# A macaron encoder layer on one core: another order of seven products, six plain tiles, an embedding norm elsewhere, other first loads

## The chip, the core and the metric

The kernel runs on one core of a Trainium2 chip. The metric is the time of one execution on the device in microseconds (us). The engines are named TensorE (PE in the profile, its weight loads PEld), VectorE (DVE), ScalarE (ACT), GpSimd (POOL) and SyncE (SP, which only issues DMAs here).

## What is computed

One layer of a bidirectional encoder for 512 positions of width 1024, all in fp32:

```python
h = h + 0.5 * swiglu(rms_norm(h, g_ffn1), w_ffn1_gate, w_ffn1_up, w_ffn1_down)   # width 2816
u = rms_norm(h, g_mix) @ w_in
h = h + concat([o_mla(u), o_diff(u)]) @ w_out
h = h + 0.5 * swiglu(rms_norm(h, g_ffn2), w_ffn2_gate, w_ffn2_up, w_ffn2_down)
gate = sigmoid(rms_norm(h, g_ple_in) @ w_ple_gate + b_ple_gate)
h = h + gate * rms_norm(p @ w_ple_proj, g_ple_out)
```

swiglu is (silu(u @ w_gate) * (u @ w_up)) @ w_down. The change touches the two feed-forward blocks, the product p @ w_ple_proj (the embedding product), its norm, and the start.

## The kernel before

**Precision.** Each fp32 operand is split into a high part (a cast to fp32r on ScalarE) and a low part (a subtraction on VectorE); `split`, lines 91 to 93. One product is three matmuls: high by high, high by low, low by high (`mm3`, lines 250 to 253). Everything is held transposed: features on the partitions, the 512 positions along the columns, so h is 8 tiles of 128x512.

**Weights.** All weights lie in one stream, read in order. `load_chunk` (line 106) loads a block of 128x1024 (512 KB) on SP's queue and splits it; there are 3 raw buffers and 5 of split blocks. `load_unit` (line 118) makes seven weight forms out of two such blocks, with two DMAs that add into SBUF (issued by GpSimd, lines 127 and 128) and two sums on GpSimd (lines 131 and 132): xa holds the blocks A11 and A12, xb S1 and A22, xc S3, xs S2 and S4. `nxt` (line 138) keeps about three blocks, or one unit, loaded ahead.

**Feed-forward block** (`ffn`, line 397). The 22 tiles of 128 inner columns come in three groups, `FGROUPS` (line 23): first tile, tiles, plain tiles. A plain tile is 24 matmuls of 512 columns for the gate and 24 for the up product (`proj`). The other tiles come in pairs: a pair is two runs of `seven` (line 359), one for the gate and one for the up product (here called the gate run and the up run). A run takes 7 products instead of 8, each of 4 x 3 matmuls of 256 columns (12). After the tiles of a group come 8 down products (`ps_d`), which are added to h.

A run of `seven` has three accumulators in PSUM, r1, r2 and r3, one bank each. A bank is read between the products that accumulate into it, and the next product into it waits for that reading. The order is

```python
mul(r1, A11, F_.B11, True, True)     # then ScalarE copies r1 to q1 lo (line 378)
mul(r3, S1, F_.N1, True, True)       # then VectorE adds r3 (line 381)
mul(r2, S2, F_.T2, True, True)       # then VectorE: q1 hi = q1 lo - r2 (line 384)
mul(r1, A12, F_.B21, False, True)
mul(r2, S3, F_.N3, False, True)      # then line 388 reads r2
mul(r3, S4, F_.B22, False, True)     # then line 391 reads r3
mul(r2, A22, F_.N4, False, True)     # then line 394 reads r2
```

The seven forms of the second operand (B11, N1, T2, B21, N3, B22, N4; class `Forms`, line 306) are built once for each block out of h, its gain and the row scale. The building is a generator of 18 steps, 9 for each half of the rows, started in the second plain tile; 6 steps are taken after each plain tile (line 453). The row scale comes from the sum of squares of h (`Norm`, line 234, summed in `square_sum`, lines 195 to 201), a reduction by matmuls (`col_rsqrt`, line 208), a power on GpSimd (line 183) and a broadcast by matmuls (`row_bcast`, line 226).

**Start.** SP's queue loads p (2 tiles), the first block of embedding weights, 4 tiles of x, the second block, 4 tiles of x, and tables. The 8 embedding products are evacuated in turn by VectorE and ScalarE into `pe` (4 pages of two tiles) and stored in DRAM. `pe_norm` (line 293) squares them on ScalarE and sums on GpSimd; it is the `side` generator of the first block, one step after each plain tile. The sum of the first norm is on VectorE (line 267). Table products for the rotary part (lines 542 to 548) are 24 small multiplications on GpSimd.

**What sets the order.** TensorE's instructions run in the order in which the code gives them. Those of the other engines are put in order by a scheduler from the code's order and their readiness; `tc.high_priority(offset=n)` moves some n places ahead. Each engine then works strictly in its order.

## Time and profile before

| | |
|---|---|
| median of 3 runs | 1090.54 us (1088.35 to 1092.55) |
| the profiled execution | 1091.32 us, its span 1089.5 us |
| TensorE busy | 1025.6 us, 94% of the span |
| VectorE, ScalarE, GpSimd busy | 69%, 47%, 29% |
| DMA | 131.25 MB, mean 120 GB/s |

The profile follows one execution. "Busy" is the time in which an engine ran an instruction; matmuls overlap, so the distance between the starts of two of them tells their pace. A timeline row gives the start, the duration, engine, line and operands, and in brackets the idle time before it with what ended it. The granted clock is the share of TensorE's full clock in a stretch; it has two levels, 1.2 and 2.4 GHz.

### The profile page before, as it was taken

To read this page: it belongs to the slowest core of one execution; us is meant where nothing else is said; L and a number is where in the kernel's file an instruction comes from. 1 tells how busy PE (TensorE), PEld (TensorE's weight loads), DVE (VectorE), ACT (ScalarE), POOL (GpSimd) and SP (SyncE) were. 2 spreads that over 40 slices of the span, in tenths; PEclk is the share of its full clock that TensorE was granted. 3 is DMA by queue.
4 is the path that set the end of the run, shared out by engine and by line. 5 is a ranking of instruction groups with operands and counts; after the bars stand their busy time and mean duration, and the time that the engine had idled before them with its cause. 6 is when DMAs were issued, how large, how long until landed. Compare 5 with 4: busy or idle time off the path is not lost.

```text
span 1089.5 us, 15824 instructions
## 1 busy us (share of the span) xinstructions
PE 1025.6 (94%) x6056; PEld 898.4 (82%) x6056; DVE 750.3 (69%) x1216; ACT 509.2 (47%) x811; POOL 317.3 (29%) x304
## 2 busy tenths in 40 slices
PE   7788999999999999998889999969999999999998
PEld 5677989998898989886458888869889998999886
DVE  7488735886368656888878865887537874487673
ACT  8444423544144444657787744443325442344441
POOL 2743113340134030004454314332023511241330
PEclk9897999999999999999899999979999999999999
DMA  8524643766355443221200023335636655364441
GB/s 313 172 68 107 173 124 106 173 151 194 97 132 139 146 165 104 86 98 58 78 20 1 21 66 100 91 101 132 178 79 163 165 163 139 106 162 115 136 149 49
DMA packets 47580, 131.25 MB, mean 120 GB/s; under 512 B 5520, under 2 KB 6160, under 8 KB 47504
## 3 DMA queue, kind: packets, MB, share of 16 engines
q1 hardware_dynamic: 34560, 105.04, 29.6%
q0 software_dynamic: 11648, 23.07, 11.9%
q10 hardware_dynamic: 1296, 2.13, 0.5%
q8 instruction: 47, 0.77, 0.3%
q14 instruction: 29, 0.24, 0.1%
HBM read 123.93 MB, written 6.29 MB: 120 GB/s over the span
## 4 chain that ended last, share of the span: by engine, by line
PE 73%; DVE 13%; issue 5%; ACT 4%; DMA 3%; POOL 2%; SPq 0%; ACTq 0%; POOLq 0%; DVEq 0%
PE r L251 9%; PE r L252 8%; PE r L253 8%; PE ps_d L252 7%; PE ps_d L251 7%; PE ps_d L253 7%; PE ps_in L251 2%; PE ps_in L253 2%; PE ps_in L252 2%; DMA rc<-in_wst_dram 2%; DVE y L328 1%; DVE xb L93 1%; PE ps_pg L251 1%; PE ps_pg L253 1%; PE ps_wo L251 1%
## 5 line engine op out<-in xcount | busy, mean ns | idle before, releaser
L92 ACT CAST hl<-raw 128x1024 fp32r<-128x1024 f32 (+4 forms) x100 | 98.9, 992 | 167.0 <-issue 72.9
L93 DVE TENSOR_TENSOR hl<-raw,hl 128x1024 fp32r<-128x1024 f32 (+4 forms) x100 | 116.3, 1166 | 45.4 <-ACT hl L92 45.0
L252 PE MATMUL ps_d<-ht,hl 128*128 128x512 f32 x352 | 137.2, 390 | 0.0
L251 PE MATMUL ps_d<-ht,hl 128*128 128x512 f32 x352 | 137.0, 389 | 0.0
L253 PE MATMUL ps_d<-ht,hl 128*128 128x512 f32 x352 | 136.9, 389 | 0.0
L128 POOL DMA_DIRECT2D rc<-in_wst_dram x36 | 31.2, 867 | 205.9 <-DMA rc<-in_wst_dram 132.7
L251 PE MATMUL r<-fm,xb 128*128 128x256 f32 x288 | 84.8, 295 | 5.9 <-ACT fm L92 5.9
L252 PE MATMUL r<-fm,xb 128*128 128x256 f32 x288 | 82.8, 288 | 5.6 <-DVE fm L93 5.6
L252 PE MATMUL r<-fm,xa 128*128 128x256 f32 x288 | 82.3, 286 | 3.8 <-DVE fm L93 3.8
L251 PE MATMUL r<-fm,xa 128*128 128x256 f32 x288 | 82.2, 285 | 2.6 <-ACT fm L92 2.6
L251 PE MATMUL r<-fm,xs 128*128 128x256 f32 x288 | 82.9, 288 | 0.0
L252 PE MATMUL r<-fm,xs 128*128 128x256 f32 x288 | 82.8, 288 | 0.0
L253 PE MATMUL r<-fm,xs 128*128 128x256 f32 x288 | 82.7, 287 | 0.0
L253 PE MATMUL r<-fm,xb 128*128 128x256 f32 x288 | 82.5, 287 | 0.0
L253 PE MATMUL r<-fm,xa 128*128 128x256 f32 x288 | 82.1, 285 | 0.0
L92 ACT CAST xa<-ra 128x1024 fp32r<-128x1024 f32 x36 | 37.8, 1051 | 89.9 <-PE r L253 36.1
L252 PEld LDWEIGHTS ps_d<-ht,hl 128*128 128x128 f32 x352 | 66.1, 188 | 14.1 <-DVE ht L93 0.6
L253 PEld LDWEIGHTS ps_d<-ht,hl 128*128 128x128 f32 x352 | 66.1, 188 | 13.7
L251 PEld LDWEIGHTS ps_d<-ht,hl 128*128 128x128 f32 x352 | 66.1, 188 | 13.5
L127 POOL DMA_DIRECT2D rb<-in_wst_dram x36 | 31.5, 874 | 148.7 <-DVE h L465 51.4
L92 ACT CAST xs<-ra 128x1024 fp32r<-128x1024 f32 x36 | 37.7, 1048 | 78.3 <-PE r L253 54.3
L201 POOL TENSOR_TENSOR acc<-acc,sq 128x512 f32<-128x512 f32 x21 | 34.3, 1634 | 112.8 <-ACT sq L200 112.8
(324 smaller groups left out, 2998.7 us busy)
## 6 DMA issues: line engine op xcount, KB each, us to landing
raw<-in_wst_dram SPq DMA_DIRECT2D x77, 512.0 KB, 3.5
rb<-in_wst_dram SPq DMA_DIRECT2D x36, 512.0 KB, 3.6
ra<-in_wst_dram SPq DMA_DIRECT2D x36, 512.0 KB, 3.6
rc<-in_wst_dram SPq DMA_DIRECT2D x36, 256.0 KB, 4.4
rb<-in_wst_dram POOLq DMA_DIRECT2D x36, 256.0 KB, 4.0
rc<-in_wst_dram POOLq DMA_DIRECT2D x36, 256.0 KB, 4.6
raw<-in_wst_dram SPq DMA_DIRECT2D x16, 384.0 KB, 3.1
h<-in_xT_dram SPq DMA_DIRECT2D x8, 256.0 KB, 6.7
```

What stands on the lines that cost most here:

```text
L92: nc.scalar.copy(dst_h, src)
L93: nc.vector.tensor_sub(dst_l, src, dst_h.bitcast(F32))
L127: nc.gpsimd.dma_start(out=rb[:, lo], in_=s1[:, hi], accum_op=ALU.add)
L128: nc.gpsimd.dma_start(out=rc, in_=s1[:, lo], accum_op=ALU.add)
L201: (eng or nc.gpsimd).tensor_add(acc, acc, sq)
L251: MM(ps, lhsT=wh, rhs=ah, start=start, stop=False, **kw)
L252: MM(ps, lhsT=wh, rhs=al, start=False, stop=False, **kw)
L253: MM(ps, lhsT=wl, rhs=ah, start=False, stop=stop, **kw)
L328: nc.vector.scalar_tensor_tensor(out=yk[:, j, :], in0=h[k0 + j], scalar=g(self.name, k0 + j), in1=self.rbc, op0=ALU.mult, op1=ALU.mult)
```

## The change

In words: `FGROUPS` has 6 plain tiles in its first group instead of 4, so one pair there instead of two; 4 steps of the forms' building follow each plain tile. The order of the seven is S2, A11, S1, S3, A12, S4, A22, and line 384's subtraction comes behind the copy of r1. One tile of p is loaded by ScalarE's queue; both blocks of embedding weights are loaded ahead of x, and the tables behind it. Nine matmuls of 128 columns on zeros stand ahead of the first real one. The embedding product is evacuated by VectorE alone, into passing tiles, and stored; the 4 pages `pe` are gone. Its norm is the `side` of the second block, one step after each down product of the first two groups, and loads the tiles again from DRAM by GpSimd's queue. The first norm's sum is on GpSimd. The 24 table products are 6 larger ones.

```diff
@@ -20,7 +20,7 @@
 DFF = 2816
 NF = DFF // P
 
-FGROUPS = ((0, 8, 4), (8, 8, 0), (16, 6, 0))
+FGROUPS = ((0, 8, 6), (8, 8, 0), (16, 6, 0))
 HS = S // 2
 NH = 8
 NOPE = 64
@@ -148,7 +148,7 @@
 
     pTs = [t2(f"pT{k}") for k in range(2)]
     for k in range(2):
-        nc.sync.dma_start(out=pTs[k], in_=pT[k])
+        (nc.sync, nc.scalar)[k].dma_start(out=pTs[k], in_=pT[k])
     cst = const.tile([P, NCC], F32, name="cst")
     gc = const.tile([P, NGC], F32, name="gc")
     nc.scalar.dma_start(out=gc, in_=gcols)
@@ -163,6 +163,11 @@
     warm = const.tile([P, 1], F32, name="warm")
     nc.vector.memset(warm, 0.0)
     nc.scalar.activation(warm, warm, AF.Silu)
+    zero = t2("zero")
+    nc.vector.memset(zero[:, :P], 0.0)
+    pw = psum("pw")
+    for _ in range(9):
+        MM(pw[:, :P], lhsT=zero[:, :P], rhs=zero[:, :P], start=True, stop=True)
     h = pairs("h")
     row = const.tile([P, 320], F32, name="row")
     ident = cst[:, CC["ident"]:CC["ident"] + P]
@@ -259,42 +264,38 @@
             mm3(ps, w[:, 0, c], w[:, 1, c], acts[k][:, 0, :], acts[k][:, 1, :], k == 0, k == n - 1)
 
 
+    load_chunk((256, 512))
     pact = []
     for k in range(2):
         a = page(f"pact{k}")
         split(a[:, 0, :], a[:, 1, :], pTs[k])
         pact.append(a)
-    n1 = Norm("ffn1", nc.vector)
-    pe = pairs("pe")
+    n1 = Norm("ffn1")
     pe_dram = drp.tile([KT, P, S], F32, name="pe_dram")
     rpe = const.tile([P, TT], F32, name="rpe")
-    load_chunk((256, 512))
+    load_chunk((512,))
+    for t in range(KT):
+        nc.sync.dma_start(out=h[t], in_=xT[t])
+    nc.sync.dma_start(out=cst, in_=consts)
+    nc.sync.dma_start(out=row, in_=rows.partition_broadcast(P))
     for half in range(2):
         ms = range(4 * half, 4 * half + 4)
-        for t in ms:
-            nc.sync.dma_start(out=h[t], in_=xT[t])
-        if half == 0:
-            load_chunk()
-        else:
-            nc.sync.dma_start(out=cst, in_=consts)
-            nc.sync.dma_start(out=row, in_=rows.partition_broadcast(P))
-        for t in ms:
-            n1.add(t)
         w = ready.pop(0)[1]
         for m in ms:
+            n1.add(m)
             ps = psum("ps_pe")
             proj(ps, w, pact, (m % 4) * 2)
-            if m % 2:
-                nc.vector.tensor_copy(out=pe[m], in_=ps)
-            else:
-                nc.scalar.copy(pe[m], ps)
-            nc.gpsimd.dma_start(out=pe_dram[m], in_=pe[m])
+            pe = t2("pe")
+            nc.vector.tensor_copy(out=pe, in_=ps)
+            nc.gpsimd.dma_start(out=pe_dram[m], in_=pe)
 
     def pe_norm():
         pe_acc = t2("pe_acc")
         for m in range(KT):
-            square_sum(pe_acc, pe[m], m == 0)
-        yield
+            pe = t2("pel")
+            nc.gpsimd.dma_start(out=pe, in_=pe_dram[m])
+            square_sum(pe_acc, pe, m == 0)
+            yield
         r4 = col_rsqrt(pe_acc, DM)
         nc.vector.tensor_copy(out=rpe, in_=r4)
         yield
@@ -373,19 +374,18 @@
                 mm3(r[:, lo], x[:, 0, c], x[:, 1, c], bh, bl, start and k == 0, stop and k == 3,
                     skip_group_check=True)
 
+        mul(r2, S2, F_.T2, True, True)
         mul(r1, A11, F_.B11, True, True)
         with tc.high_priority(offset=150):
             nc.scalar.copy(q1[:, lo], r1[:, lo])
+            nc.vector.tensor_sub(q1[:, hi], q1[:, lo], r2[:, lo])
         mul(r3, S1, F_.N1, True, True)
         with tc.high_priority(offset=150):
             nc.vector.tensor_add(q2[:, lo], r3[:, lo], q1[:, lo])
-        mul(r2, S2, F_.T2, True, True)
-        with tc.high_priority(offset=150):
-            nc.vector.tensor_sub(q1[:, hi], q1[:, lo], r2[:, lo])
-        mul(r1, A12, F_.B21, False, True)
         mul(r2, S3, F_.N3, False, True)
         with tc.high_priority(offset=150):
             nc.vector.tensor_sub(q3[:, hi], r2[:, lo], q2[:, lo])
+        mul(r1, A12, F_.B21, False, True)
         mul(r3, S4, F_.B22, False, True)
         with tc.high_priority(offset=150):
             nc.vector.tensor_add(q2[:, hi], r3[:, lo], q1[:, hi])
@@ -448,9 +448,7 @@
                     first = (psg, psu, hts)
                 else:
                     evac(psg, psu, hts)
-                if side is not None:
-                    next(side, None)
-                for _ in range(6):
+                for _ in range(4):
                     if builder is not None:
                         next(builder, None)
             if builder is not None:
@@ -466,6 +464,8 @@
                                                op0=ALU.mult, op1=ALU.add)
                 if gi == len(FGROUPS) - 1:
                     after(m)
+                elif side is not None:
+                    next(side, None)
 
     nmix = Norm("mix")
     h_dram = drp.tile([KT, P, S], F32, name="h_dram")
@@ -474,7 +474,7 @@
         nmix.add(m)
         nc.scalar.dma_start(out=h_dram[m], in_=h[m])
 
-    ffn(n1, after1, pe_norm())
+    ffn(n1, after1)
 
 
     deferred = []
@@ -539,13 +539,13 @@
     HR = ROPE // 2
     nc.vector.tensor_scalar_mul(row[:, :ROPE], row[:, :ROPE], 2.0 ** -0.5)
     for i in range(2):
-        gr = row[:, i * ROPE:(i + 1) * ROPE]
+        def gr(lo, hi):
+            return row[:, i * ROPE + lo:i * ROPE + hi].unsqueeze(1).broadcast_to([P, TT, hi - lo])
         cosv = cst[:, CC["cos"]:CC["cos"] + TT * ROPE].rearrange("p (t r) -> p t r", r=ROPE)
         sinv = cst[:, CC["sin"]:CC["sin"] + TT * ROPE].rearrange("p (t r) -> p t r", r=ROPE)
-        for tt in range(TT):
-            nc.gpsimd.tensor_mul(trig[:, 2 * i, tt, :], cosv[:, tt, :], gr)
-            nc.gpsimd.tensor_mul(trig[:, 2 * i + 1, tt, :HR], sinv[:, tt, :HR], gr[:, HR:])
-            nc.gpsimd.tensor_mul(trig[:, 2 * i + 1, tt, HR:], sinv[:, tt, HR:], gr[:, :HR])
+        nc.gpsimd.tensor_mul(trig[:, 2 * i], cosv, gr(0, ROPE))
+        nc.gpsimd.tensor_mul(trig[:, 2 * i + 1, :, :HR], sinv[:, :, :HR], gr(HR, ROPE))
+        nc.gpsimd.tensor_mul(trig[:, 2 * i + 1, :, HR:], sinv[:, :, HR:], gr(0, HR))
     lam = const.tile([P, 4], F32, name="lam")
     lt = const.tile([P, 64], F32, name="lt")
     for i in range(2):
@@ -971,7 +971,7 @@
 
 
     n3 = Norm("ple_in")
-    ffn(n2, n3.add)
+    ffn(n2, n3.add, pe_norm())
     pe2 = []
     for m in range(KT):
         if m % 2 == 0:
```

## Rows read from the trace of the kernel before

**Rows 1.** Who TensorE waited for, the whole run: line, releaser, us in total, times, longest
```profile
PE r L251 <- DVE q L384: 15.1, 13, 1.8
PE r L252 <- DVE fm L93: 9.4, 4, 3.3
...
PE ps_bc L205 <- POOL r L183: 6.8, 1, 6.8
```

**Rows 2.** Stages: us, busy us (instructions) per engine, granted clock, DMA share, GB/s
```profile
76.20:97.00 20.80, 11.92 (x67) 10.90 (x67) 18.57 (x24) 8.75 (x15) 9.11 (x7) 0.67 0.29 66
...
173.40:260.00 86.60, 82.95 (x673) 81.44 (x672) 64.64 (x86) 38.53 (x56) 30.52 (x25) 1.00 0.58 153
...
710.50:730.00 19.50, 10.41 (x53) 9.40 (x52) 17.90 (x22) 7.07 (x13) 8.59 (x7) 0.65 0.32 69
```

**Rows 3.** Order of time on TensorE: start us, us, what; start to first down product
```profile
5.33 0.80 PE L251 MATMUL ps_pe<-pact,hl 128*128 128x512 f32 x1 [5.33 <-ACT hl L92]
...
21.80 0.39 PE L251 MATMUL ps_g<-act_ffn,hl 128*128 128x512 f32 x1
...
131.36 0.40 PE L251 MATMUL ps_d<-ht,hl 128*128 128x512 f32 x1
```

**Rows 4.** Stages: the first loads, and the plain tiles of the second block
```profile
10.00:15.00 5.00, 3.19 (x13) 1.99 (x11) 4.99 (x8) 4.67 (x8) 0.79 (x2) 1.00 0.98 340
...
688.00:710.50 22.50, 22.50 (x101) 18.62 (x100) 21.46 (x26) 10.69 (x16) 8.41 (x7) 1.00 0.36 94
```

**Rows 5.** Order of time on ScalarE in a pair: a cast of 1024 columns
```profile
212.85 1.05 ACT L92 CAST xs<-ra 128x1024 fp32r<-128x1024 f32 x1 [1.60 <-PE r L253]
```

**Rows 6.** Order of time on VectorE behind the start of a later pair
```profile
199.87 1.21 DVE L93 TENSOR_TENSOR xb<-rb,xb 128x1024 fp32r<-128x1024 f32 x1
201.01 0.41 DVE L381 TENSOR_TENSOR q<-r,q 128x256 f32<-128x256 f32 x1
...
201.94 0.41 DVE L384 TENSOR_TENSOR q<-q,r 128x256 f32<-128x256 f32 x1
```

**Rows 7.** Groups by line and shape: fp32 matmuls; busy us, mean ns
```profile
L871 PE MATMUL ps_do<-ptd,vd 128*128 128x512 f32 x32 | 17.4, 628 | 2.8 <-ACT ptd L905 2.8
```

**Rows 8.** Line 201, the sums of squares: ns min, median, max
```profile
L201 POOL TENSOR_TENSOR acc<-acc,sq x21: 1288/1588/1859, 378.9 to 1040.8; 128x512 f32<-128x512 f32 x21
L201 DVE TENSOR_TENSOR acc<-acc,sq x7: 685/686/689, 10.7 to 22.7; 128x512 f32<-128x512 f32 x7
L201 POOL TENSOR_TENSOR pe_acc<-pe_acc,sq x7: 1250/1288/2753, 26.4 to 43.8; 128x512 f32<-128x512 f32 x7
```

**Rows 9.** Groups of GpSimd by line and shape: busy us, mean ns
```profile
L291 POOL DMA_DIRECT2D pe_dram<-pe x8 | 4.6, 576 | 20.4 <-DVE pe L288 15.9 <-ACT pe L290 4.5
...
L546 POOL TENSOR_TENSOR trig<-cst,row 128x32 f32<-128x32 f32 x8 | 4.2, 519 | 0.1
```

**Rows 10.** Order of time on TensorE, second block
```profile
665.57 0.39 PE L251 MATMUL ps_g<-act_ffn,hl 128*128 128x512 f32 x1
...
676.45 0.95 PE L211 MATMUL ps_ss<-cst,acc 128*128 128x1 f32 x8
...
768.07 0.40 PE L251 MATMUL ps_d<-ht,hl 128*128 128x512 f32 x1
```

**Rows 11.** Order of time on TensorE, the first run of a later pair
```profile
195.40 0.28 PE L251 MATMUL r<-fm,xa 128*128 128x256 f32 x1
...
199.72 0.28 PE L251 MATMUL r<-fm,xa 128*128 128x256 f32 x1
...
202.40 0.38 PE L251 MATMUL r<-fm,xc 128*128 128x256 f32 x1 [1.08 <-DVE q L384]
```

**Rows 12.** Order of time on ScalarE in the same run: the copy of r1
```profile
197.04 0.37 ACT L378 COPY q<-r 128x256 f32<-128x256 f32 x1 [0.39 <-PE r L253]
```

**Rows 13.** Order of time on TensorE behind another wait for line 384
```profile
751.94 0.38 PE L251 MATMUL r<-fm,xc 128*128 128x256 f32 x1 [1.81 <-DVE q L384]
...
755.39 0.41 PE L253 MATMUL r<-fm,xs 128*128 128x256 f32 x1
```

## The prediction

> **What bounds the kernel now.** I read the page first, then who TensorE waited for over the whole run, then a table of stages, then the order of time where a stage had idle time. On the page TensorE is busy through nearly the whole span, so only its idle time and its slow time can be won. Three kinds of wait hold most of it [rows 1]: products waiting for the forms of their second operand (9.4 us on VectorE's half of them alone), the products S3 waiting for the subtraction in line 384 (15.1 us in 13 waits), and one wait of 6.8 us for a reciprocal root on GpSimd. The stage table puts the first two at the change from plain tiles to products in both feed-forward blocks: 11.92 us busy of 20.80 in one, 10.41 of 19.50 in the other, both with a granted clock of about two thirds [rows 2]. That is the lower of the two levels (1.2 GHz) for some 13 us each, so the idle time is paid again in slow matmuls. The middle row there holds the four pairs of the second group: full clock, and 3.65 us idle in three waits for line 384.
>
> The steps are priced on one profiled execution of 1091.32 us (span 1089.5); the median of the runs shown is 1090.54, so 0.8 us less. A measurement of this kernel can tell about 0.5% from no change, which is 5.5 us.
>
> **First loads, zeros, embedding product.** The first feed-forward matmul starts at 21.80 [rows 3]. Ahead of it go 0.5 MB of p, two weight blocks of 0.5 MB, 2 MB of x, 0.8 MB of tables and one more block: 4.85 MB. At the 340 GB/s of the stage from 10 to 15 us [rows 4] this takes 14.3 us, plus some 2 us until the queues are full; the cast and the subtraction of that last block (1.05 and 1.21 us, by blocks of the same shape in [rows 5, 6]) end near 18.5, and with half a microsecond of queueing the stage starts at 19.0. Gain 2.8. Nothing here comes earlier than the 48 matmuls of the embedding product at 0.227 us after a start at 6.3, so 4.5 is the most; the least is nothing, if VectorE, busy 4.99 us of 5.00 in that stage, stays the bound (it loses seven sums of 0.69 us to GpSimd and gains four evacuations of about the same). The nine zero matmuls are no rows here. An fp32 matmul of 512 columns has two records of 628 ns [rows 7], which overlap; a quarter of the columns at half the clock is between 0.3 and 0.6 us each, 2.8 to 5.7 us from about 1.1 us on. The first real matmul came at 5.33, 0.80 us long where later ones take 0.39 [rows 3], so the zeros end between 1.4 us before it and 1.5 us after. I take no cost and no gain beyond the start above. One copy of p on ScalarE's queue saves one issue on SP and delays only the gains table, needed later.
>
> **The 6.8 us wait.** GpSimd was still summing squares of the embedding product (seven sums of 1250 to 2753 ns [rows 8], with 24 small table products between) in front of the root that feeds the row scale, and TensorE stood. The change takes those sums out of this block. What comes next in their place is the sum of the first norm, which moves from VectorE (686 ns each) to GpSimd (1588 ns median [rows 8]). Seven of these, eight store issues of 0.58 us and six table products of 0.52 us [rows 9] are 19 us from some 9 on, done near 28; the root is needed only after three half tiles, near 36. So the wait goes whole. In the second block the embedding sums, eight loads and eight squares stand in the down products of the first group, 42 us long, where VectorE and ScalarE are half idle; the 2 MB read twice are hidden there, and the root there comes one group later. Cover gone, the 11 us of sums would delay the next weight unit.
>
> **Six plain tiles.** In the first block group 0 ran from 21.80 to the first down product at 131.36, 109.6 us; in the second from 665.57 to 768.07, 102.5 us [rows 3, 10]. One plain tile is 48 matmuls in 10.88 us (665.57 to 676.45), 0.2267 each. Six are 65.3. A product of the seven is 12 matmuls in 1.44 us (36 from 195.40 to 199.72 in [rows 11]), so a pair is 14 products, 20.2, and 0.1 at its seams. Norm reductions and row broadcast: 0.95 [rows 10] and about 0.5. Sum 86.9 if the forms are there in time. Two more plain tiles for one pair fewer thus cost 1.5 us of matmul time, and are paid by cover. The forms were late because their building filled VectorE: 21.46 us of 22.50 [rows 4], with the last six of 18 steps behind the evacuation of the last plain tile. Now they are 4 steps a tile over five tiles, 20 calls for 18 steps; only the last two forms (B22, N4) come behind the last evacuation, and these are used 7 and 8.6 us into the first product run. In the second block VectorE had 21.46 + 17.90 us of work from 688 to 730 [rows 2, 4]; with four more block splits and two more evacuations of four steps (some 10 us) and without the 3 us that belong to the product run it is 46, in the 47 us between the row scale and the first product. So it remains nearly full; I leave 1.5 us of waiting (0 to 6). That makes 88.4: gains of 21.2 and 14.1 us. They contain the wait of 6.8, the slow clock after each stall, and one wait for line 384 each, since only the first pair of group 0 is left.
>
> **The order of the seven.** Left over are ten gate runs (second and later pairs of groups 1 and 2, both blocks), whose waits hold 12.3 of the 15.1 us (1.1 and 1.7 go with group 0). In one of them product A11 starts at 195.40, and S3 could start after four products at 201.16; it starts at 202.40, behind line 384, which VectorE does last in a backlog of the pair before: the split of xb at 199.87, line 381 at 201.01, a split, line 384 at 201.94 [rows 6, 11]. In the new order line 384 needs no third product, but it needs the copy of r1 by ScalarE (0.20 us after the product, 0.37 long [rows 12]), and S3 comes after three products, at 199.72 in this run. Put in the place of line 381 it ends at 201.37: a wait of 1.65 instead of 1.24. Put ahead of the xb split the wait is 0.5; left where it was, at 202.35, it is 2.6. The place of line 381 is nearest, since the copy and line 381's product end within half a microsecond of each other. Ten times 1.65 is 16.5: a cost of 4.2 us. The other spacing is looser: A22 has two products' time behind line 388 instead of one. The weights xs come first now, and their buffer is freed by A12, fifth instead of fourth: from there 2.88 us and two matmuls until they are needed. The chain is 0.2, a cast of 1.05 and a subtraction of 1.2 us [rows 5, 6], 2.45 us: it fits by about half a microsecond. I take no cost.
>
> **Sum.** 2.8 + 21.2 + 14.1 - 4.2 = 33.9; 1091.3 - 33.9 = 1057.
>
> **The rivals.**
> A, the new order frees the S3 wait (16%). If line 384 comes before the split of xb and finds VectorE free, 12.3 us go too: 1057 - 16.5 = 1041. For it: each accumulator is read with two products' time to spare. Against: the copy of r1 now stands in the chain.
> B, each S3 wait grows and TensorE's clock falls behind it (18%). A wait of 1.81 us at 751.94 was followed by matmuls of 0.41 instead of 0.28 us, the lower level: 17 in 3.45 us up to 755.39 [rows 13] where 2.04 would do, 1.4 us lost. The three waits of the stage from 173.4 to 260 us, 1.1 to 1.3 us each, were not (clock 1.00 [rows 2]). With 2.6 us for each wait and the fall behind most of them, 10 x (2.6 + 1.2) = 38 instead of 16.5: 1078.
> C, group 0 still waits for its forms (10%): half of the idle time (18 us in two stages of [rows 2]) and of the slow time behind it (some 8) stays, 13 us, less 3 counted: 1067. For it: VectorE stays full.
> D, the row scale is late again (4%). With the longest sum of [rows 8], 2753 ns, for all seven, and twice the means of [rows 9] for the rest, GpSimd ends near 44 instead of 28 and TensorE waits some 8 us, and loses 1.4 in slow matmuls: 1066. The medians speak against it.
> The Trainium skill (GPSIMD Engine Reference, 4.1 Engine selection) advises VectorE for elementwise work on a tile, GpSimd being about twice as slow with two inputs. By that rule the moved sum is D's mechanism; the trace agrees in price, 1588 against 686 ns, and does not show it on the path.
> E, slower than before (6%): xs late at every product run. If the xs split falls behind two other splits on VectorE (1.2 us each) and the freed buffer also delays the next load, S2 waits. There are 26 runs with a predecessor to free that buffer. It decides from 33.9 / 26 = 1.3 us a run on; at 2.4 us less the half microsecond of slack, and 1.4 us of slow clock behind half of them, it gives 1057 + 26 x 2.6 = 1125. Against it: in this trace ScalarE starts xs within 0.3 us of the free buffer.
> That the change doesn't do what it says could be so for the first loads alone, if they leave SP's queue in the old order: at most 3 us, within the range.
>
> **How the numbers follow.** The forecast, with S3 waits of 1.1 to 2.3 us, a start between 17.4 and 21.8 and up to 6 us for forms, has 46% and runs from 1050 to 1066. Half of A, two thirds of B, and C and D with it reach 1041 to 1078; what is left out is half of A, a third of B and all of E, about 2 in 10. Faster by over 0.5% are the forecast, A, and nearly all of B, C and D: 92%. Within 0.5%: a tail of C and B and the mild end of E, 4%. Slower by over 0.5%: E, 4%.
>
> **What would show it.** Right: the first feed-forward matmul near 19; no wait for the GpSimd root; the first down product of the two blocks 88 us after the first gate product; a granted clock of 1.00 around the first pair; ten waits of S3 near 1.65 us, now behind a chain of copy and subtraction. Wrong: waits of S2 for xs at the start of each run (E), lower clock after the S3 waits (B), no S3 waits at all (A), or product waits for forms again (C).

## The result, and the profile after

The changed kernel is slower: 1106.69 us median of 4 runs (1104.23 to 1108.55) against 1091.54 for the kernel before beside it; ratio 1.0142, 95% interval 1.0112 to 1.0173, well beyond the half per cent that can be told from no change. The forecast was 1057, its range 1041 to 1078. The profiled execution took 1106.54 us, its span is 1104.7, mean granted clock 0.976.

Who TensorE waited for, the whole run of the changed kernel (line, releaser, us in total, times, longest); line 381 there is line 384 of before, the subtraction that gives q1 hi:

```profile
PE r L256 <- DVE q L381: 44.4, 22, 3.7
PE ps_g L258 <- DVE hl L93: 6.5, 1, 6.5
```

Against [rows 1], the waits for the forms and the 6.8 us for the root are gone. The wait of S3 has grown from 15.1 us in 13 places to 44.4 in 22, and there is a new one of 6.5 us in the first feed-forward tile. Where each is, in order of time on TensorE (start, duration, what, and in brackets the idle time before it):

```profile
20.11 0.50 PE L256 MATMUL ps_g<-act_ffn,hl 128*128 128x512 f32 x1 [0.36 <-ACT hl L92]
...
27.30 0.79 PE L258 MATMUL ps_g<-act_ffn,hl 128*128 128x512 f32 x1 [6.45 <-DVE hl L93]
27.89 0.63 PE L256 MATMUL ps_g<-act_ffn,hl 128*128 128x512 f32 x1
...
121.58 0.40 PE L256 MATMUL ps_d<-ht,hl 128*128 128x512 f32 x1
...
181.12 0.39 PE L256 MATMUL r<-fm,xc 128*128 128x256 f32 x1 [1.42 <-DVE q L381]
...
193.64 0.39 PE L256 MATMUL r<-fm,xc 128*128 128x256 f32 x1 [2.19 <-DVE q L381]
...
671.14 0.39 PE L256 MATMUL ps_g<-act_ffn,hl 128*128 128x512 f32 x1
...
763.04 0.40 PE L256 MATMUL ps_d<-ht,hl 128*128 128x512 f32 x1
```

Set beside [rows 3, 10]: from the first gate product to the first down product it was 109.6 us and is 101.5 in the first block (88.4 forecast), and was 102.5 and is 91.9 in the second (88.4 forecast). So group 0 gained, less than forecast. The row at 181.12 is an up run's S3, the one at 193.64 a gate run's. In groups 1 and 2 of both blocks the up run of every pair but a group's last waits so, 1.2 to 2.9 us, and the gate run of every pair but a group's first, about 2.2 us: ten waits of each kind. The other two waits, 3.66 and 3.36 us, are in the only pair of group 0 of each block.

The loss stands in groups 1 and 2. Their four stretches of `seven` in the kernel before (us, busy us and instructions per engine, granted clock, DMA share, GB/s):

```profile
174.90:261.00 86.10, 82.45 (x674) 81.20 (x673) 65.40 (x87) 39.53 (x57) 29.23 (x24) 1.00 0.59 155
304.40:368.40 64.00, 61.68 (x506) 60.90 (x506) 47.00 (x64) 28.40 (x42) 18.62 (x15) 1.00 0.52 140
811.60:897.20 85.60, 82.38 (x674) 81.12 (x673) 65.59 (x87) 39.75 (x57) 29.23 (x24) 1.00 0.60 158
940.70:1005.50 64.80, 61.69 (x506) 60.84 (x505) 47.11 (x64) 28.40 (x42) 18.63 (x15) 1.00 0.53 139
```

And in the changed kernel:

```profile
165.10:261.30 96.20, 83.85 (x674) 82.60 (x674) 64.89 (x86) 39.47 (x56) 27.56 (x23) 0.98 0.53 140
304.70:373.60 68.90, 61.65 (x506) 60.80 (x505) 47.06 (x64) 28.42 (x42) 18.11 (x15) 1.00 0.47 125
807.70:905.00 97.30, 86.73 (x674) 85.49 (x673) 66.25 (x86) 39.49 (x56) 29.41 (x26) 0.95 0.53 141
949.30:1021.20 71.90, 64.64 (x507) 63.79 (x506) 47.32 (x64) 28.40 (x42) 18.21 (x15) 0.95 0.46 120
```

The same matmuls take 334.3 us instead of 300.5: 33.8 us, where the prediction allowed 4.2. The waits for line 381 in these stretches are 44.4 - 3.66 - 3.36 = 37.4 us, against 12.2 us of waits for line 384 before (15.1 less the two in group 0, 1.10 and 1.81); that is 25 of the 33.8. TensorE's busy time grew by 296.87 - 288.20 = 8.7 us with no matmul more: that goes with the granted clock of 0.95 and 0.98.

VectorE's order says why S3 waits. First an up run of the changed kernel, whose S3 could have started at 179.70, then a gate run, whose S3 could have started at 191.45 (start of the product less its wait):

```profile
176.84 2.21 DVE L93 TENSOR_TENSOR xb<-rb,xb 128x1024 fp32r<-128x1024 f32 x1
178.97 1.76 DVE L93 TENSOR_TENSOR xc<-rc,xc 128x512 fp32r<-128x512 f32 x1
180.66 0.41 DVE L381 TENSOR_TENSOR q<-q,r 128x256 f32<-128x256 f32 x1
...
189.73 1.79 DVE L428 TENSOR_TENSOR q<-q,q 128x512 f32<-128x512 f32 x1
191.44 1.21 DVE L93 TENSOR_TENSOR xb<-rb,xb 128x1024 fp32r<-128x1024 f32 x1
192.58 0.68 DVE L93 TENSOR_TENSOR ht<-a,ht 128x512 fp32r<-128x512 f32 x1
193.18 0.41 DVE L381 TENSOR_TENSOR q<-q,r 128x256 f32<-128x256 f32 x1
```

The copy of r1, on which line 381 depends, in the same two runs on ScalarE, and then the start of the gate run's product A11, which it copies:

```profile
178.30 0.37 ACT L380 COPY q<-r 128x256 f32<-128x256 f32 x1 [0.21 <-PE r L258]
...
192.60 0.36 ACT L380 COPY q<-r 128x256 f32<-128x256 f32 x1
```

```profile
188.41 0.28 PE L256 MATMUL r<-fm,xa 128*128 128x256 f32 x1
```

In the up run the copy was done 2.0 us ahead of line 381; what held the subtraction was its place, behind the splits of xb and xc, 3.9 us together. Ahead of the xc split it would have been done near 179.4, in time for 179.70. In the gate run three things come together. VectorE has a backlog up to the end of the xb split (192.65), which is already 1.2 us late; then comes a half tile's split (ht); and the copy itself, behind three casts on ScalarE, ends at 192.96, only 0.2 us ahead of the subtraction.

### The profile page after: what moved, and what is told of

Read it like the earlier page. It is cut to its first block, busy times and chain, and to the rows that moved or that the text cites. A ratio compares the mean times of both kernels' runs of the same rounds, so it can differ in the third digit from the quotient of the medians.

```text
span 1104.7 us, 15452 instructions
## 1 busy us (share of the span) xinstructions
PE 1035.2 (94%) x5930; PEld 900.6 (82%) x5930; DVE 741.1 (67%) x1193; ACT 501.0 (45%) x794; POOL 303.3 (27%) x285
## 4 chain that ended last, share of the span: by engine, by line
PE 68%; DVE 18%; issue 5%; DMA 4%; ACT 4%; POOL 1%; SPq 0%; ACTq 0%; POOLq 0%; DVEq 0%
PE ps_d L257 7%; PE ps_d L258 7%; PE ps_d L256 7%; PE r L256 6%; PE r L258 5%; PE r L257 5%; DMA rc<-in_wst_dram 3%; DVE xb L93 2%; PE ps_in L256 2%; PE ps_in L258 2%; PE ps_in L257 2%; DVE q L428 2%; DVE xa L93 1%; DVE fm L93 1%; PE ps_g L258 1%
## 5 line engine op out<-in xcount | busy, mean ns | idle before, releaser
L92 ACT CAST hl<-raw 128x1024 fp32r<-128x1024 f32 (+4 forms) x109 | 107.6, 989 | 145.0 <-issue 44.5
L93 DVE TENSOR_TENSOR hl<-raw,hl 128x1024 fp32r<-128x1024 f32 (+4 forms) x109 | 126.0, 1158 | 41.2 <-ACT hl L92 40.9
L256 PE MATMUL r<-fm,xc 128*128 128x256 f32 x128 | 41.4, 323 | 44.4 <-DVE q L381 44.4
L257 PEld LDWEIGHTS ps_d<-ht,hl 128*128 128x128 f32 x352 | 66.1, 188 | 15.6 <-DVE ht L93 1.9
L206 POOL TENSOR_TENSOR acc<-acc,sq 128x512 f32<-128x512 f32 x28 | 43.3, 1546 | 117.2 <-ACT sq L205 117.0
L256 PE MATMUL r<-fm,xa 128*128 128x256 f32 x256 | 74.7, 292 | 0.0
L257 PE MATMUL r<-fm,xa 128*128 128x256 f32 x256 | 74.5, 291 | 0.0
L258 PE MATMUL r<-fm,xa 128*128 128x256 f32 x256 | 74.3, 290 | 0.0
L93 DVE TENSOR_TENSOR xs<-ra,xs 128x1024 fp32r<-128x1024 f32 x32 | 39.2, 1225 | 50.6 <-ACT xs L92 31.7
L257 PE MATMUL r<-fm,xs 128*128 128x256 f32 x256 | 72.9, 285 | 0.0
L128 POOL DMA_DIRECT2D rc<-in_wst_dram x32 | 27.8, 889 | 164.3 <-DMA rc<-in_wst_dram 108.8
L256 PE MATMUL r<-fm,xs 128*128 128x256 f32 x256 | 72.9, 285 | 0.0
L258 PE MATMUL r<-fm,xs 128*128 128x256 f32 x256 | 72.8, 284 | 0.0
L256 PE MATMUL r<-fm,xb 128*128 128x256 f32 x256 | 72.4, 283 | 0.0
L257 PE MATMUL r<-fm,xb 128*128 128x256 f32 x256 | 72.4, 283 | 0.0
L258 PE MATMUL r<-fm,xb 128*128 128x256 f32 x256 | 72.4, 283 | 0.0
L256 PEld LDWEIGHTS r<-fm,xc 128*128 128x128 f32 x128 | 26.9, 210 | 48.9 <-DVE q L381 48.9
```

The costliest lines, as they stand in the source:

```text
L92: nc.scalar.copy(dst_h, src)
L93: nc.vector.tensor_sub(dst_l, src, dst_h.bitcast(F32))
L128: nc.gpsimd.dma_start(out=rc, in_=s1[:, lo], accum_op=ALU.add)
L206: (eng or nc.gpsimd).tensor_add(acc, acc, sq)
L256: MM(ps, lhsT=wh, rhs=ah, start=start, stop=False, **kw)
L257: MM(ps, lhsT=wh, rhs=al, start=False, stop=False, **kw)
```

## The experiments

All times are medians; ratios are to the kernel before, run beside each. Theory 1 says that the order of the seven is what costs, and the rest of the change gains.

**1. The changed kernel with the old order of the seven.**

```diff
-        mul(r2, S2, F_.T2, True, True)
         mul(r1, A11, F_.B11, True, True)
...
-            nc.vector.tensor_sub(q1[:, hi], q1[:, lo], r2[:, lo])
         mul(r3, S1, F_.N1, True, True)
...
+        mul(r2, S2, F_.T2, True, True)
+        with tc.high_priority(offset=150):
+            nc.vector.tensor_sub(q1[:, hi], q1[:, lo], r2[:, lo])
+        mul(r1, A12, F_.B21, False, True)
         mul(r2, S3, F_.N3, False, True)
...
-        mul(r1, A12, F_.B21, False, True)
```

> The changed kernel with the seven products in their old order again (A11, S1, S2, A12, S3, S4, A22); everything else of the change stays. Theory 1, the order is what costs: groups 1 and 2 of both blocks go back to their old lengths, together some 33 us shorter than in the changed kernel, and the first pair of group 0 loses some 3 us of waiting in each block: 1106.5 - 33 - 6 = about 1067. Rival, the order is innocent and something else in the change (norm sums on GpSimd, other buffers, more weight blocks to split) slowed groups 1 and 2: the waits move to another line, and the time stays at 1095 to 1107.

Measured: 1070.87 us, ratio 0.9817 (0.9795 to 0.984). S3 waits 18.9 us in 14 places instead of 44.4 in 22, up runs mostly without, and the four stretches of groups 1 and 2 are 301.0 us together, the 300.5 of before again. Theory 1 holds: the rest of the change gains about 20 us, and its order of the seven takes 36 back.

**2. The kernel before with the new order alone**, the edit of experiment 1 the other way round:

```diff
+        mul(r2, S2, F_.T2, True, True)
         mul(r1, A11, F_.B11, True, True)
...
-        mul(r2, S2, F_.T2, True, True)
...
-        mul(r1, A12, F_.B21, False, True)
         mul(r2, S3, F_.N3, False, True)
...
+        mul(r1, A12, F_.B21, False, True)
```

> The kernel before with nothing changed but the order of the seven products (S2 first, line 384 behind the copy of r1). Theory 1, the order is what costs: S3 waits of about 2.2 us in gate runs and 1.4 us in up runs, all over groups 1 and 2 and in the four pairs of group 0: 1091.5 + 33 for groups 1 and 2 + some 6 for group 0 = about 1130. Rival, the order costs only together with the rest of the change: 1091 to 1096.

Measured: 1128.55 us, ratio 1.0351 (1.0325 to 1.0376). Waits for the subtraction of q1 hi (line 380 in this kernel) and for the forms (rows as in the first fence):

```profile
PE r L251 <- DVE q L380: 43.5, 24, 2.2
PE r L251 <- ACT fm L92: 18.9, 2, 9.7
```

The order costs 38 us by itself. Part of it is not the subtraction: S2 needs the third form, T2, and now wants it first. The wait for the forms' high halves was 8.5 us in four places before; that for their low halves fell from 9.4 to 5.8, so the forms' waits grew by 6.8 us together.

**3. S3 behind A12 in the changed kernel.**

```diff
+        mul(r1, A12, F_.B21, False, True)
         mul(r2, S3, F_.N3, False, True)
...
-        mul(r1, A12, F_.B21, False, True)
```

> The changed kernel with S3 and A12 exchanged: S2, A11, S1, A12, S3, S4, A22. The chain of line 381 (copy of r1, subtraction, behind the splits of VectorE) stays as it is, but has one product more, 1.44 us, before S3 needs it. If the waits are a matter of VectorE's backlog and not of the chain's own length, up-run waits (1.42 us) go whole, gate-run waits fall from 2.19 to about 0.75, those of the first pairs from 3.5 to 2: 10 x 1.42 + 10 x 1.44 + 2 x 1.44 = 31 us and some of the slow clock behind them: about 1070. Rival: the subtraction is in program order behind work that itself waits for a later product (so it moves with S3), and the waits stay: 1100 to 1107.

Measured: 1067.83 us, ratio 0.9796 (0.9778 to 0.9814). The waits for the subtraction are gone. In their place:

```profile
PE r L256 <- ACT q L380: 16.4, 12, 3.0
```

A12 adds into r1 and so waits for the copy of r1; this happens in the ten gate runs (1.04 to 1.26 us) and the first pairs. There the copy stands on ScalarE behind the cast of a half tile, which itself waits for VectorE's multiplication of the pair before (line 428). The time came out as expected, the place of the remaining waits did not.

**4. The old order, with the first norm's sums on VectorE.** To the edit of experiment 1 comes

```diff
-    n1 = Norm("ffn1")
+    n1 = Norm("ffn1", nc.vector)
```

> The changed kernel with the old order of the seven, and the sums of the first norm back on VectorE as in the kernel before. Against the old order alone: if GpSimd's sums stretch VectorE's work in the first 27 us (8 subtractions of line 249, four of them 1.25 to 4.43 us long beside line 206), the third feed-forward matmul comes some 4 us earlier and the time falls by 3 to 5. Rival: VectorE's order (norm splits ahead of the first weight block's) is what delays it; then seven sums of 0.69 us come in front too and it starts some 4 us later, and the time rises by 2 to 5.

Measured: 1066.12 us, ratio 0.9788 (0.9763 to 0.9814); against experiment 1 the intervals overlap. In the trace the stretch of the norm subtractions is gone. Line 249 in the changed kernel and in this one (ns min, median, max; first and last start):

```profile
L249 DVE SCALAR_TENSOR_TENSOR act_ffn<-h,gc,act_ffn x8: 740/1262/1897, 13.6 to 23.7; 128x512 fp32r<-128x512 f32 x8
```

```profile
L249 DVE SCALAR_TENSOR_TENSOR act_ffn<-h,gc,act_ffn x8: 742/746/747, 12.0 to 21.4; 128x512 fp32r<-128x512 f32 x8
```

The median falls from 1.26 to 0.75 us. But the seven sums of 0.69 us take the room, and the first weight block's split starts at 23.28 instead of 23.55 in experiment 1. The third feed-forward matmul comes 0.8 us earlier (24.55 against 25.39), not the 4 us of the first expectation, so its reason does not hold though its time does; the rival's rise does not come at all. (The 4.43 us in the expectation is a row of four subtractions; the longest single one takes 1.90.) The wait at the start is a matter of how much stands ahead of that split, and moving the sums to GpSimd freed VectorE of only about 1.3 us (4.8 us of sums less 3.5 of stretch).

**5. The old order (as in experiment 1), and four plain tiles with six steps each.**

```diff
-FGROUPS = ((0, 8, 6), (8, 8, 0), (16, 6, 0))
+FGROUPS = ((0, 8, 4), (8, 8, 0), (16, 6, 0))
-                for _ in range(4):
+                for _ in range(6):
```

> The changed kernel with the old order of the seven (the base, 1070.9) and four plain tiles with six builder steps each in group 0, as in the kernel before. The prediction's own working puts the six tiles at 21.2 + 14.1 us, of which 6.8 are the wait for the root that this kernel does not have either: 1070.9 + 28.5 = 1099. Rival: with GpSimd free of the embedding sums and of 18 table products, the forms come earlier even with four tiles, and the tiles are worth only the slow clock and some idle time: 1080 to 1088.

Measured: 1087.06 us, ratio 0.9979 (0.9967 to 0.9991). Six tiles are worth 16 to 18 us (1087.06 - 1070.87 by the medians, 17.7 by the two ratios), not 28.5. The waits for forms are back, 19.8 us where before had 17.9:

```profile
PE r L256 <- DVE q L385: 13.9, 13, 1.3
PE r L256 <- ACT fm L92: 11.5, 4, 4.9
PE r L257 <- DVE fm L93: 8.3, 4, 2.3
```

So the rival's reason (earlier forms) is wrong, though its size is nearer: its 1080 to 1088 holds the time by luck. What is given back stands in the first pair: with six tiles its S3 waits 3.60 and 2.85 us (experiment 1), and slow matmuls follow; with four the first pair waits for forms and its S3 not at all.

**6. The old order without the matmuls on zeros.**

```diff
-    zero = t2("zero")
-    nc.vector.memset(zero[:, :P], 0.0)
-    pw = psum("pw")
-    for _ in range(9):
-        MM(pw[:, :P], lhsT=zero[:, :P], rhs=zero[:, :P], start=True, stop=True)
```

> The same base (old order, 1070.9) without the nine matmuls on zeros. Theory: the start of the feed-forward block is set by VectorE's splits, so the zeros change nothing there: 1069 to 1073. Rival 1: without them the embedding product runs at the lower clock for longer and the sixteen half blocks of work behind it shift: 1072 to 1075. Rival 2: they hold the first real matmul up: 1068 or less.

Measured: 1071.18 us, ratio 0.983 (0.981 to 0.9851). No difference to experiment 1 that can be measured; the theory holds.

**7. The order A11, S2, S1, A12, S3, S4, A22 in the changed kernel.**

```diff
+        mul(r1, A11, F_.B11, True, True)
+        with tc.high_priority(offset=150):
+            nc.scalar.copy(q1[:, lo], r1[:, lo])
         mul(r2, S2, F_.T2, True, True)
-        mul(r1, A11, F_.B11, True, True)
         with tc.high_priority(offset=150):
-            nc.scalar.copy(q1[:, lo], r1[:, lo])
             nc.vector.tensor_sub(q1[:, hi], q1[:, lo], r2[:, lo])
         mul(r3, S1, F_.N1, True, True)
...
+        mul(r1, A12, F_.B21, False, True)
         mul(r2, S3, F_.N3, False, True)
...
-        mul(r1, A12, F_.B21, False, True)
```

> The changed kernel with the order A11, S2, S1, A12, S3, S4, A22: the copy of r1 has two products before A12 overwrites r1, and the subtraction of line 381 has two products before S3. Base for comparison: S3 moved behind A12 (1067.8), where the gate runs wait 1.05 us for the copy, in ten places, and the first pairs 2.8. Theory, the waits are cover too short for a backlog of about 1 to 2 us: gate-run waits fall to 0 to 0.4, first pairs to 1.5: 1067.8 - 9 - 3 = about 1057. Rival: the subtraction lands behind the same pair tail as in the old order, with the same one product of cover left, and ten waits of 1.1 us stay: 1068 to 1071.

Measured: 1056.23 us, ratio 0.9695 (0.968 to 0.9709), as the theory has it. Of the waits for line 381 (382 here) five are left, and in groups 1 and 2 together they are 0.7 us (the other two are in group 0, 1.93 and 1.31):

```profile
PE ps_g L258 <- DVE hl L93: 5.4, 1, 5.4
PE r L256 <- DVE q L382: 4.0, 5, 1.9
```

**8. Experiment 4 with the first feed-forward block loaded and split between the halves of x.**

```diff
     for t in range(KT):
+        if t == KT // 2:
+            load_chunk()
         nc.sync.dma_start(out=h[t], in_=xT[t])
```

> The changed kernel with the old order and the first norm's sums on VectorE (the base, 1066.1), and the first feed-forward weight block loaded and split between the two halves of x, as in the kernel before. Theory, it is VectorE's order that holds the third feed-forward matmul (split of the low half at 23.3 us, behind eight norm splits): the split comes at about 15, the 6.3 us of waiting at the first tile shrink to 2 or less, now for norm splits, and some slow clock goes: about 1060. Rival, it is VectorE's volume (over 95% busy from 5 to 26 us), so the wait only moves to the later norm splits: 1065 to 1067.

Measured: 1062.72 us, ratio 0.9754 (0.974 to 0.9767), about 3.5 us below experiment 4. TensorE's waits in the first tiles are two instead of one, 1.1 us for a norm split and 1.1 for the next block's:

```profile
PE ps_u L258 <- DVE hl L93: 1.1, 1, 1.1
PE ps_g L257 <- DVE act_ffn L249: 1.1, 1, 1.1
```

In experiment 4 the waits there were 4.3 us for the block's split and 2.0 for its cast; the order was the cause of most of that, 6.3 against 2.2 us, and VectorE's volume takes over with the rest: both expectations were half right. The first pair and group 1 of the first block gave some of it back (in group 1 4.82 us idle instead of 3.23).

**9. The first two products exchanged, nothing else:** A11, S2, S1, S3, A12, S4, A22. The edit is the upper half of that of experiment 7:

```diff
+        mul(r1, A11, F_.B11, True, True)
+        with tc.high_priority(offset=150):
+            nc.scalar.copy(q1[:, lo], r1[:, lo])
         mul(r2, S2, F_.T2, True, True)
-        mul(r1, A11, F_.B11, True, True)
         with tc.high_priority(offset=150):
-            nc.scalar.copy(q1[:, lo], r1[:, lo])
             nc.vector.tensor_sub(q1[:, hi], q1[:, lo], r2[:, lo])
```

> The changed kernel with its first two products exchanged and nothing else: A11, S2, S1, S3, A12, S4, A22. S3 keeps the fourth place and its subtraction one product (S1) of cover; only the copy of r1 leaves the end of the chain, for it has S2 as cover. In VectorE's written-out order the subtraction then stands ahead of the xc split in up runs, and ahead of the first half tile's split (0.6 us) in gate runs, where in the changed kernel it stands behind them. Theory, the copy in the chain is what set the subtraction's place: up-run waits go from 1.42 to 0, gate-run waits from 2.19 to about 1.6, and some of the slow clock goes with them: 10 x 1.42 + 10 x 0.6 + 2 x 0.6 = 21, with 5 to 10 of clock: 1076 to 1086. Rival, three products are too early for any subtraction whatever its place (VectorE's backlog alone): both waits stay above 1 us, 1095 to 1107.

Measured: 1072.14 us, ratio 0.9837 (0.982 to 0.9853). The same two runs as shown above for the changed kernel, on VectorE (line 382 is line 381 there):

```profile
175.84 2.21 DVE L93 TENSOR_TENSOR xb<-rb,xb 128x1024 fp32r<-128x1024 f32 x1
177.97 0.41 DVE L382 TENSOR_TENSOR q<-q,r 128x256 f32<-128x256 f32 x1
178.30 1.45 DVE L93 TENSOR_TENSOR xc<-rc,xc 128x512 fp32r<-128x512 f32 x1
...
188.76 1.21 DVE L93 TENSOR_TENSOR xb<-rb,xb 128x1024 fp32r<-128x1024 f32 x1
189.89 0.41 DVE L382 TENSOR_TENSOR q<-q,r 128x256 f32<-128x256 f32 x1
190.22 0.68 DVE L93 TENSOR_TENSOR ht<-a,ht 128x512 fp32r<-128x512 f32 x1
```

One place further ahead in each run. Of the ten up runs one still waits for it, 0.25 us; the ten gate runs wait 1.51 to 1.59 us. Waits for the subtraction fall from 44.4 to 22.2 us, and the granted clock of groups 1 and 2 is 1.00 again in all four stretches, where TensorE's busy time is 286.2 us instead of 296.9: with the waits nearly all of the 34.6 us won. The time is 4 us below the theory's range. This is the sharpest of the runs, since S3 keeps its place and its cover. In the up runs the copy at the end of the chain set the subtraction's place in VectorE's order, and the place set the wait. In the gate runs place and copy account for 0.6 of the 2.19 us; the other 1.6 is VectorE's backlog ahead of the subtraction, which this exchange leaves, and there the rival is right.

**10. The kernel before with the order of experiment 7 alone.**

```diff
         mul(r1, A11, F_.B11, True, True)
...
+        mul(r2, S2, F_.T2, True, True)
+        with tc.high_priority(offset=150):
+            nc.vector.tensor_sub(q1[:, hi], q1[:, lo], r2[:, lo])
         mul(r3, S1, F_.N1, True, True)
...
-        mul(r2, S2, F_.T2, True, True)
-        with tc.high_priority(offset=150):
-            nc.vector.tensor_sub(q1[:, hi], q1[:, lo], r2[:, lo])
         mul(r1, A12, F_.B21, False, True)
```

> The kernel before with nothing changed but the order A11, S2, S1, A12, S3, S4, A22. The order alone, without the rest of the change, takes away most of the 15.1 us of waits for line 384 and the slow clock behind a few: by the difference that it made on the changed kernel (1070.9 to 1056.2) 1091.5 - 14.6 = about 1076. Rival: without the rest, the late forms of group 0 shift what VectorE does and part of the waits stays: 1080 to 1086.

Measured: 1080.75 us, ratio 0.9912 (0.9897 to 0.9926): the rival's time, for another reason than it gave. The waits for line 384 (381 here) are all but gone, 0.7 us in four places, but those for the forms and the root grew, by 4.3 us (8.5, 9.4 and 6.8 before):

```profile
PE r L251 <- ACT fm L92: 10.8, 4, 5.5
PE r L252 <- DVE fm L93: 9.6, 4, 3.4
PE ps_bc L205 <- POOL r L183: 8.6, 1, 8.6
```

**11 and 12. Everything that gained.** Experiment 7 with the sums on VectorE and the early block; then also every second copy of the embedding product on ScalarE:

```diff
-            nc.vector.tensor_copy(out=pe, in_=ps)
+            if m % 2:
+                nc.vector.tensor_copy(out=pe, in_=ps)
+            else:
+                nc.scalar.copy(pe, ps)
```

> The changed kernel with the order A11, S2, S1, A12, S3, S4, A22, the first norm's sums on VectorE and the first feed-forward weight block between the two halves of x. If the three gains add up (14.6 for the order, 4.7 for the sums, 3.4 for the block, from 1070.9): 1048. Rival, the sums' gain and the block's gain are the same time counted twice, or the wait returns in the norm splits: 1051 to 1054.

> As the kernel of the run before, with every second evacuation of the embedding product on ScalarE, as the kernel before had it: four copies of 0.68 us less on VectorE between 8 and 24 us, where it is the bound. If VectorE's volume holds the first feed-forward tile, up to 2.7 us come off: about 1046. Rival: ScalarE is itself busy with squares and casts there, and the copies delay the norm products by as much: 1048 or more.

Measured: 1051.06 us, ratio 0.9643 (0.9628 to 0.9657), and 1049.16 us, ratio 0.9626 (0.9611 to 0.964). The gains at the start do not add up in full: the first time is the rival's of experiment 11, and the second the rival's of experiment 12. The copies' 1.9 us lie within overlapping intervals. TensorE is busy 98% of the last one's span, granted clock 0.993. Either is some 5% below the changed kernel.

## Why the prediction was wrong, step by step

The forecast and the profiled execution are 49 us apart. Of these 29.6 are the order of the seven in groups 1 and 2 (33.8 against 4.2), 13.1 and 3.5 the two groups 0 (101.5 and 91.9 against 88.4), and 1.1 the start (20.11 against 19.0). Most of the other 2 are in the down products of the second block.

**The order of the seven failed, as a term of the sum.** It stood at 4.2 us and measured 33.8 in groups 1 and 2. Three things were missed.
- "Left over are ten gate runs." Ten up runs wait too. The prediction looked at one gate run and took the up runs as free. Even before, one of them waited: the waits left in groups 1 and 2 were eleven, 12.2 us, ten in gate runs and one in an up run.

```profile
979.28 0.39 PE L251 MATMUL r<-fm,xc 128*128 128x256 f32 x1 [0.77 <-DVE q L384]
```

  And the trace of before held the rows that tell it: in the up run that starts at 185.13, line 384 ended 5.4 us after the start,

```profile
185.13 0.28 PE L251 MATMUL r<-fm,xa 128*128 128x256 f32 x1
```

```profile
188.76 1.45 DVE L93 TENSOR_TENSOR xc<-rc,xc 128x512 fp32r<-128x512 f32 x1
190.13 0.41 DVE L384 TENSOR_TENSOR q<-q,r 128x256 f32<-128x256 f32 x1
```

  while S3 in the new order is due after three products, 4.3 us. Left at its old place the wait is 1.1 us; measured 1.42 or 1.47 in eight of ten, 15.6 us in all. A cover of four products (5.76 us) hid a chain of 5.4 us, one of three does not.
- "The place of line 381 is nearest": 1.65 us a gate run, between 0.5 and 2.6. It is 2.19, for the half tile's split came in front. The bounds held, the choice did not: 5 us. The copy of r1 had been taken to start 0.20 us behind its product, as in [rows 12]; in the gate run above it starts 2.75 us behind (192.60; A11 started at 188.41 and takes 1.44). Had the subtraction stood ahead of the half tile's split, that would still have left 0.3 of the 0.6 us between 2.19 and 1.58. Experiment 9, where the copy has one product more of cover, comes near the forecast: 1.58.
- The sum had nothing for the lower clock behind the longer waits; rival B had. TensorE's busy time grew 8.7 us: behind six of the ten gate runs' waits the matmuls were slow for a while, behind none of the up runs'. B's mechanism was right. For the ten gate runs its price, 38 us, was above what they cost (21.9 of waits and 8.7 of clock); but it too left out the up runs, 15.6 us, and its 1078 kept the forecast's other terms.

Two readings in that part are off by little, and change nothing: by its row line 381 ends at 201.42, not 201.37, and the two waits of group 0 are 1.10 and 1.81 us, so that 12.2 of the 15.1 are left, not 12.3.

**First loads.** The gain of 2.8 was taken from the first matmul, and that came at 20.11 (19.0 forecast), 1.7 us earlier. But the third, the first to need the low half, came at 27.30, and the pace stayed at the lower level until some 4 us later. That the cast and the subtraction of the last block end near 18.5 failed: the cast ended at 20.07, the subtraction began at 25.45, behind eight norm subtractions and eight copies. VectorE as the bound was named, with no gain as its worst; but it is a loss: [rows 4] showed VectorE full, and the changed order put 16 instructions ahead of the one that TensorE needs. Experiment 8 takes most of that back.

**The 6.8 us wait** went whole, as forecast. Its price was hidden, though: the sums moved to GpSimd stretch what VectorE does beside them (experiment 4).

**Six plain tiles.** The waits for forms went whole; 1.5 us had been left for them. "One wait for line 384 each" was taken off; the one left, in the first pair, is 3.66 and 3.36 us, behind the same full VectorE queue, and the lower clock follows it. So a part of the forms' backlog was not covered but moved to the next wait. In the second block this makes the missing 3.5 us (91.9 against 88.4), since the 1.5 were left over; in the first the 6.5 us of the start and its slow matmuls come on top: its plain tiles take 75.9 us, those of the second block 66.7.

**Zeros, embedding norm, xs first** cost next to nothing, as forecast: experiment 6 for the zeros; the embedding norm's reduction now takes 0.94 us of TensorE in the second block's down products, at 910.34, and the first block is without it. Among TensorE's waits in the changed kernel none is for the embedding norm's root and none for xs, so rival E's mechanism is not there, though its sign was. E looked at the right place, splits in front of something short of time on VectorE, and at the wrong instruction.

**The rivals.** A's free S3 came only with other orders (experiments 3, 7 and 10), C's waits for forms only with four plain tiles (experiments 2, 5 and 10). The Trainium skill's rule (GPSIMD Engine Reference, 4.1 Engine selection) spoke for leaving the sum on VectorE. Its price was right (1.3 us a sum beside 0.69), and D's mechanism, a late root, did not come: GpSimd's last sum ended at 26.2. What the sum on GpSimd did cost, VectorE's own time, stood in neither.

## What to carry to other kernels

When a product is brought forward, measure the whole chain from the start of the run to the end of what releases it, in every kind of run, those that do not wait today above all: a run without a wait only says that its cover is longer than its chain. On an engine that works strictly in its order, what matters for a short instruction is which long ones stand ahead of it, and an input that comes later, as the copy of r1 did here, can put it behind one more. Of several orders with the same arithmetic, try the one that gives the early reads of the accumulators two products before the next write: here, with two for the first read of each of r1, r2 and r3, 1056 us against 1107, by the order of the first products and of S3 and A12 alone. Its last read, between S3 and A22, has only S4 as cover and held one run, for 0.4 us. Which orders do better on another kernel was not tested.

## What the runs showed of the hardware

**VectorE beside GpSimd.** VectorE's subtractions with two operands in SBUF stretch while GpSimd adds; its copies out of PSUM don't. From the changed kernel, VectorE and then GpSimd in the same two microseconds:

```profile
21.28 0.68 DVE L289 COPY pe<-ps_pe 128x512 f32<-128x512 f32 x1
21.88 1.27 DVE L249 SCALAR_TENSOR_TENSOR act_ffn<-h,gc,act_ffn 128x512 fp32r<-128x512 f32 x1
```

```profile
21.31 1.28 POOL L206 TENSOR_TENSOR acc<-acc,sq 128x512 f32<-128x512 f32 x1
```

The copy lies beside the sum but for its first 0.03 us and takes its usual 0.68 us; the subtraction overlaps it by 0.71 us and takes 0.53 more than the 0.74 of experiment 4. The eight subtractions are 9.2 us busy in the changed kernel and 5.7 in experiment 4, so the seven sums (4.8 us), moved to GpSimd, took 3.5 us back. The Trainium skill (SBUF — State Buffer, "Who interferes with whom") says that a VectorE instruction with two SBUF inputs contends with a GpSimd instruction that reads SBUF, and that one with at most one SBUF input, outside certain modes, does not; the traces agree, with these numbers. The xb split of 2.21 us in the up run above, 1.21 in the gate run, looks like the same thing (GpSimd's sums of lines 131 and 132 run beside the first and not beside the second); that was not tested by itself.

**The clock behind short waits.** A wait of 2.19 us at 193.64 was followed by matmuls of 0.28 us, the full level (2.4 GHz). The same wait at 243.71 was followed at once by the lower one (1.2 GHz; granted clock 0.62 from 243.7 to 248.2):

```profile
243.71 0.55 PE L256 MATMUL r<-fm,xc 128*128 128x256 f32 x1 [2.19 <-DVE q L381]
244.05 0.42 PE L257 MATMUL r<-fm,xc 128*128 128x256 f32 x1
...
247.24 0.28 PE L257 MATMUL r<-fm,xa 128*128 128x256 f32 x1
```

Of the ten gate runs' waits of 2.17 to 2.19 us in the changed kernel six were followed by the lower level, three of them only 1.4 to 1.6 us after S3 had started; of the ten up runs' waits none was, not even one of 2.89 us at 231.19. With waits of 1.5 to 1.6 us in every gate run but the first of a group (experiment 9) the clock did not fall in any of the four stretches. Why one wait of 2.19 us costs 1.5 us by slow matmuls and the next one nothing is left open.
